# Query transposes for two heads at once and three moves of the order, in an encoder layer with attention and a state space

## The chip, the cores and the metric

The kernel runs on one core of one Trainium2 chip. The metric is the device time of one execution in microseconds (us), from several runs of the same program. Engines are named as in the profile: PE (TensorE; its weight loads stand apart as PEld), DVE (VectorE), ACT (ScalarE), POOL (GpSimd) and SP (SyncE, which here only issues transfers).

## The reference, cut to what matters

Two sequences of 512 tokens (1024 channels each, float32) go through one encoder layer: a projection, a windowed attention and a state-space branch side by side, a gated sum, and an MLP. The part that the change touches is the attention's queries:

```python
q = rms_norm(q.reshape(bsz, seq_len, N_HEADS, HEAD_DIM), q_gain)      # 16 heads of 64
k = rms_norm(k.reshape(bsz, seq_len, N_KV_HEADS, HEAD_DIM), k_gain)   # 4 key heads, 4 query heads each
s = jnp.einsum('nqkgd,njkd->nkgqj', qb, kw) * scale + bias            # a block of 128 queries, 3 blocks of keys
s = jnp.where(mask, s, NEG_INF)
p = softmax(concat([s, sink_col]))[..., :-1]
o = jnp.einsum('nkgqj,njkd->nqkgd', p, vw)
```

## The kernel before, in words

**Precision.** A float32 matmul is made of products of two rounded parts, high and low: each operand is split by ACT (a cast to the rounded type, the high part) and DVE (a subtraction, the low part).

**Stages around the change.** First the state-space scan, beside which PE computes gate columns. Then the *read-out* (lines 911 to 942): 32 iterations `q`, each with `turn_states` (copies on ACT and DVE), `read_out` (six matmuls of 128x128 on PE, lines 858 and 860), the load of tables for five iterations later (`tables_in`, on SP), pieces of other PE work (`work`: the last two gate columns in 12 pieces, then the key projection of 8 tiles in 16 pieces), and `gelu` (ACT, line 868), which frees the product's bank; there are two such banks. A table `casts` (line 906) says in which iterations a piece of the key weights (`w_k.piece`) or value weights (`w_v.piece`) is loaded (SP, line 717), cast (ACT, line 718) and subtracted (DVE, line 719). The pieces go through two raw buffers (`c_raw`). The first key product comes in iteration 14, by `until = (q + 1) * len(work) // NQ`, and with it the first two pieces are needed; pieces two and three are needed in iteration 15.

**Attention** (lines 953 to 1367). The loop runs over 8 steps (key head `j`, sequence `sq`); a step has four query blocks `qb` of 128 tokens. A `Unit` is one query block with its four heads: `scores` (two matmuls a head, of the queries against high and low keys), `largest` (DVE, line 1052: adds the bias and takes the row's maximum), `exp` (ACT, line 1058), then, one block later, `turn` (four transposes of p a key block, line 1064), `high` (ACT, line 1068), `low` (DVE, line 1073) and `value` (line 1080) for two or three key blocks, and `lower_part` and `add`. A block at the sequence's edge has two key blocks, others three; `n3` is their number for the block being finished, so it is 3 in the third and fourth blocks of a step (`qb` 2 and 3) and 2 in the first and second.

Beside a Unit the loop makes one `Tile` of the next step's queries: `project` (24 matmuls of 128x256 in parts of 8, 4, 2, 4, 4 and 2, line 724), `square` (ACT), `power` (DVE and POOL, lines 1005 to 1008), `norm`, `turn`, `high` and `low`, the last four one block later under the name `rows`. `norm` (DVE, line 1012) writes the normalized queries of four heads, and POOL (line 1013) copies them, so that each head stands twice, side by side. `turn` (line 1018) transposes each doubled head, 128x128, which puts a head's 64 channels twice under each other. `high` (ACT, line 1023) writes the scaled high part to both halves; `low` (DVE, line 1027) puts the low part over the lower half (partitions 64 to 127). One matmul then multiplies high and low queries with keys that stand twice as well. There are 32 tiles: three are finished before the loop (`entry`), the fourth in the first block of the first step, the others in the loop.

In a step's first block `key_copies` (POOL, line 972) and `key_turn` (lines 981 to 983) make the next step's keys ready, with PE, ACT and DVE in that order. In the second block `Divide` brings the row sums. In most steps a piece of the next query weights is loaded, cast and subtracted (lines 717 to 719) in two of the blocks; one step, in which all of them are in, has none.

**Order.** In read-out and attention the order on PE, ACT and DVE is that of the program text (`manual_schedule`), in attention POOL's too. An engine works in this order, and an instruction that waits holds all behind it. SP's order is not written out there: a planner issues a transfer where, by its own reckoning, the buffer is free.

Of the kernel before, what the change touches and what calls it, by code (L numbers as in the profile page):

```python
# [11 lines left out]
F32 = mybir.dt.float32  # L12
F32R = mybir.dt.float32r
I32 = mybir.dt.int32
AF = mybir.ActivationFunctionType
ALU = mybir.AluOpType
AX = mybir.AxisListType

P = 128
# [10 lines left out]
G = 4  # L30
HD = 64
# [32 lines left out]
def hybrid_layer(ctx, tc, x, xT, rel, onehot, early, w_qkv, w_ug, q_gain, k_gain, sink,  # L64
                 b_re, b_im, c_re, c_im, d_skip, w_glu, b_glu, w_out, ln2, w_up, w_down, out):
    nc = tc.nc
    V, S, PE, GP, SP = nc.vector, nc.scalar, nc.tensor, nc.gpsimd, nc.sync
# [12 lines left out]
    def acc():  # L80
        return ps_acc.tile([P, 512], F32, tag="acc", name="acc")
# [22 lines left out]
    ident = const.tile([P, P], F32, name="ident")  # L104
# [4 lines left out]
    gain_q = const.tile([P, 1], F32, name="gain_q")  # L109
# [161 lines left out]
    with tc.tile_pool(name="xin", bufs=2, reuse_waits="tile") as xin, tc.tile_pool(name="ssmc", bufs=1) as sc:  # L271
# [10 lines left out]
        rows, columns, first_w = {}, {}, []  # L282
# [191 lines left out]
        for n in (1, 2, 4):  # L474
            a, b = slice(1, n + 1), slice(n + 1, 2 * n + 1)
# [46 lines left out]
    if True:  # L522
        h = hp.tile([P, NCHUNK, 2, GROUPS, NSEQ], F32, name="h")
        GP.memset(h[:, 0], 0.0)

        with tc.tile_pool(name="ssmt", bufs=2) as sp:
# [64 lines left out]
            def turn(q, gp):  # L591
                bm = turned[gp] = sp.tile([P, 2, SH, P], F32, tag="bm", name="bm")
                ps = tps()
                for i in range(4):
                    PE.transpose(ps[:, i * P:(i + 1) * P],
                                 made[q][0][:, i // SH, gp * SH + i % SH].rearrange("p t c -> p (t c)"), ident)
                S.copy(bm.rearrange("p r g n -> p (r g n)"), ps)
# [56 lines left out]
            for q in range(NQ4):  # L654
                more = q + 1 < NQ4
                if q % 2 and more:
                    coefficients((q + 1) // 2)
                if q:
                    lags_out(q - 1)
                table_out(q)  # L660
                for gp in range(2):
                    turn(q, gp)
                if q % 2 == 0 and q:
                    lag_weights(q // 2)
                pay(act_owed)
                pay(cast_owed)
                if more:
                    tables(q + 1)
                run(3)
                pay(dve_owed)  # L670
                for gp in range(2):
                    states(q, gp)
                    if more:
                        inputs_in(q + 1, gp)
                lags(q)
                run(3)
                pay(act_owed)
                pay(dve_owed)
                if q % 2 and (q + 3) // 2 < KT:
                    bc_tiles[(q + 3) // 2] = b_and_c((q + 3) // 2)  # L680
# [88 lines left out]
    w_k = Block(w_qkv[K_BLK], [(knp, ("x_hi", "x_lo")), column])  # L769
    w_v = Block(w_qkv[V_BLK], [column, (evp, ("ev", "ev"))])  # L770

    with tc.tile_pool(name="ssmo", bufs=2, reuse_waits="tile") as sp:
# [129 lines left out]
        def last_cast():  # L902
            cast_owed.pop(0)()
            return dve_owed.pop()

        casts = {0: [last_cast], 1: [last_cast], 2: [lambda: w_k.piece(0)], 3: [lambda: w_k.piece(1)], 8: [lambda: w_k.piece(2)], 9: [lambda: w_k.piece(3)],
                 17: [lambda: w_v.piece(0)], 18: [lambda: w_v.piece(1)], 20: [lambda: w_v.piece(2)], 21: [lambda: w_v.piece(3)]}

        scan()
# [43 lines left out]
    with tc.tile_pool(name="att", bufs=2, reuse_waits="tile") as ap:  # L953
        steps = [(j, sq) for j in range(N_KV) for sq in range(NSEQ)]
        weights, keys, queries, biases = {0: w_q0}, {}, {}, {}
# [30 lines left out]
        class Tile:  # L986
# [6 lines left out]
            def project(self, n):  # L993
                (j, sq), col = self.key, self.t * P
                weights[j].multiply(self.ps, hT[sq], col, self.k, self.k + n)
                self.k += n
# [11 lines left out]
                GP.tensor_tensor(self.rq, ms, neg_half[:, 0:G], op=ALU.pow)  # L1008

            def norm(self):  # L1010
                self.qn = ap.tile([P, G, 2, HD], F32, tag="qn", name="qn")
                V.tensor_mul(self.qn[:, :, 0], self.psv, self.rq[:, :, None].to_broadcast([P, G, HD]))
                GP.tensor_copy(self.qn[:, :, 1], self.qn[:, :, 0])

            def turn(self):
                self.pt = acc()
                for h in range(G):
                    PE.transpose(self.pt[:, h * P:(h + 1) * P], self.qn[:, h].rearrange("p a d -> p (a d)"), ident)

            def high(self):  # L1020
                self.ptv = self.pt.rearrange("p (h t) -> p h t", h=G)
                self.dst = queries[self.key][:, :, self.t * P:(self.t + 1) * P]
                S.activation(self.dst, self.ptv, AF.Copy, scale=gain_q)

            def low(self):
                dst = self.dst[64:128]
                V.scalar_tensor_tensor(dst, self.ptv[64:128], gain_q[64:128], dst.bitcast(F32),
                                       op0=ALU.mult, op1=ALU.subtract)

        class Unit:  # L1030

# [98 lines left out]
        def entry():  # L1130
            load_biases(0)
            kd = key_copies(0, 0)
            for i in range(4):
                values(i)
                w_q0.piece(i)()
            old = None
            for t in range(4):
                new = Tile(0, 0, t)
                new.project(3 * KT)
                new.square()  # L1140
                if t == 0:
                    key_turn(0, 0, kd)
                if old:
                    old.turn()
                    old.high()
                    old.low()
                if t < 3:
                    new.power()
                values(4 + t)
                if t < 3:  # L1150
                    new.norm()
                    old = new
            return new
# [45 lines left out]
        if True:  # L1199
            rows = entry()  # L1200
            for i, (j, sq) in enumerate(steps):
# [8 lines left out]
                for qb in range(NB):  # L1210
                    if 1 <= i < 3:

                        t = (i - 1) * NB + qb
# [4 lines left out]
                    n3 = prev.nkb if prev else 0  # L1218
# [54 lines left out]
                    cur.largest(3)  # L1273
                    if n3 > 2:
                        prev.turn(2)
                        prev.high(2)
                    project(4)
                    if rows:
                        rows.turn()
                    if kd:  # L1280
                        key_turn(*nxt, kd)
# [35 lines left out]
                    owed, prev, rows = prev, cur, new  # L1317
# [173 lines left out]
    with tc.tile_pool(name="glu", bufs=2, reuse_waits="tile") as gpool:  # L1491
# [11 lines left out]
        def gate_in(m, low):  # L1503
            gs_, yr, ga, at = gated[m]
            S.activation(gs_, gs_, AF.Sigmoid)
            V.tensor_mul(at, at, ga)
            low()
            V.tensor_mul(gs_, gs_, yr)
# [27 lines left out]
        for m in range(1, KT):  # L1536
            col = ahead if m == 1 else Column(m)
            for s in range(NSEQ):
                col.multiply(max((s + 1) * 3 * KT - col.i, 0))
                subs = []  # L1540
                if s == 0:
                    if 3 <= m < KT - 1:
                        split_piece()
                    if 1 < m < KT - 1:
                        w_g[m + 1], subs = column_parts(m + 1)
                ending = m == KT - 1 and s
                if ending:
                    low = late()
                gl = bank_out(m, col.ps[s])
                if not ending:  # L1550
                    low = late()
                for sub in subs:
                    sub()
                gate = m if m < 3 and s == 0 else m + 1 if s and 2 <= m < KT - 1 else 0
                if gate:
                    gate_in(gate, low)
                else:
                    low()
                if s == 0 and m < KT - 1:
                    gated[m + 1] = loads(m + 1)  # L1560
                if s and 2 <= m < KT - 1:
                    load_piece(m - 2)
                    if m == KT - 2:
                        load_piece(m - 1)
                late = lambda m=m, s=s, gl=gl: mix(m, s, gl)
                if m == KT - 1:
                    load_piece(6 + s)
# [238 lines left out]
    with tc.tile_pool(name="up", bufs=2, reuse_waits="tile") as fp:  # L1806
# [29 lines left out]
        def entry_parts():  # L1836
            raw = slot_d.tile([P, 4, 2, HALF], F32, tag="act0", name="e_raw")
            part = slot_d.tile([P, 4, 2, HALF], F32R, tag="act1", name="e_part")
            SP.dma_start(raw[:, 0], a_scr[0, :, 0:2, :])
            SP.dma_start(raw[:, 1], w_down[0, 0, :, 0:2, :])  # L1840

            def high():
                for i in range(2):
                    S.copy(part[:, 2 * i], raw[:, i])

            def low():
                for i in range(2):
                    V.tensor_sub(part[:, 2 * i + 1], raw[:, i], part[:, 2 * i].bitcast(F32))

            return high, low, [[part[:, 0], part[:, 1]], [part[:, 2], part[:, 3]]]  # L1850

        for r in range(NPAIR):
# [12 lines left out]
            if last_r:  # L1865
                w2, w3, w1, w4_, w_a22 = [lambda p=w(): p for w in (w2, w3, w1, w4_, w_a22)]
                high, low, entry_hl = entry_parts()
                final = tc.manual_schedule(engines={mybir.EngineType.PE, mybir.EngineType.Activation, mybir.EngineType.DVE})
                final.__enter__()
# [3 lines left out]
            if last_r:  # L1873
                high()
# [185 lines left out]
```

## Time and profile before

| | us |
|---|---|
| median of 3 runs | 1469.36 |
| lowest, highest | 1468.56, 1470.11 |
| the profiled execution | 1469.22 |
| its span, first to last instruction | 1467.4 |
| PE busy in the span | 1446.3 |
| DVE busy | 1094.6 |
| ACT busy | 764.2 |
| POOL busy | 168.9 |

Some 1.8 us of the execution lie outside the span. The granted TensorE clock was 0.999 of full speed over the span. A row of the profile names engine, line, operation and tiles (written <- read), the shape, a count, busy time and the mean of one in ns, and the engine's idle time before it with what ended it. A timeline row starts with start and length in us from the span's start. PE's matmuls are pipelined and their ends are modelled, so their cost is read from start to start.

### The profile page before, as it was taken

What the parts mean: (1) busy time and instruction counts of PE and PEld (TensorE: products, weight loads), DVE (VectorE), ACT (ScalarE), POOL (GpSimd) and SP (SyncE); (2) the same over time, 40 slices, a digit from 0 to 9 for tenths busy, and PEclk for the clock granted to TensorE, in tenths of its full rate; (3) what the DMA queues carried; (4) which work ended last, traced back from release to release, by engine and by line L of the source; (5) the groups of instructions that cost most, each with busy time, mean ns of one, the idle gap of its engine ahead of it and who ended that gap; (6) DMA issues with size and microseconds to landing.
All of it is one profiled execution on the core that took longest, in us unless ns stands there. A gap on an engine that the chain in (4) does not pass through costs nothing.

```text
span 1467.4 us, 21580 instructions
## 1 busy us (share of the span) xinstructions
PE 1446.3 (99%) x7782; PEld 1234.1 (84%) x7782; DVE 1094.6 (75%) x1836; ACT 764.2 (52%) x1366; POOL 168.9 (12%) x270
## 2 busy tenths in 40 slices
PE   6999999999999999999999999999999999999998
PEld 5888888888999899987888888888888888888887
DVE  7799979975636889888974689877776588575653
ACT  5489862233426778787532355554554444333332
POOL 4111120000223333343101000000000000000000
PEclk9999999999999999999999999999999999999999
DMA  8355567259941413236964134544443894454441
GB/s 300 112 171 174 161 206 268 101 178 290 307 131 35 121 46 89 95 130 217 303 212 144 72 115 165 174 149 147 155 158 123 302 346 147 158 177 153 129 129 58
DMA packets 129239, 243.86 MB, mean 166 GB/s; under 512 B 16060, under 2 KB 59324, under 8 KB 129133
## 3 DMA queue, kind: packets, MB, share of 16 engines
q1 hardware_dynamic: 104684, 186.87, 40.4%
q10 hardware_dynamic: 21888, 46.15, 8.3%
q0 software_dynamic: 2560, 9.48, 2.0%
q8 instruction: 61, 1.00, 0.3%
q14 instruction: 46, 0.37, 0.1%
HBM read 173.20 MB, written 81.82 MB: 174 GB/s over the span
## 4 chain that ended last, share of the span: by engine, by line
PE 91%; DVE 3%; ACT 2%; DMA 1%; issue 1%; POOL 1%; SPq 0%; DVEq 0%; ACTq 0%; POOLq 0%
PE bank L115 14%; PE bank L116 14%; PE bank L117 14%; PE acc L141 11%; PE acc L724 8%; PE acc L753 5%; PE acc L115 3%; PE acc L117 3%; PE acc L116 3%; PE po L1080 2%; PE sps L604 2%; PE sps L1048 2%; PE sps L860 2%; PE tps L1064 2%; PE lag L619 1%
## 5 line engine op out<-in xcount | busy, mean ns | idle before, releaser
L116 PE MATMUL bank<-b_lo,a_hi 128*128 128x512 f32 x440 | 171.2, 389 | 0.0
L117 PE MATMUL bank<-b_hi,a_lo 128*128 128x512 f32 x440 | 171.2, 389 | 0.0
L115 PE MATMUL bank<-b_hi,a_hi 128*128 128x512 f32 x440 | 171.2, 389 | 0.0
L724 PE MATMUL acc<-w_hi,hT 128*128 128x256 f32 x768 | 165.0, 291 | 0.0
L141 PE MATMUL acc<-hT,c_hi 128*128 128x512 f32 x512 | 161.1, 394 | 0.0
L1933 ACT CAST a_hi<-d_a 128x1024 fp32r<-128x1024 f32 x55 | 58.0, 1054 | 178.1 <-PE bank L116 175.2
L1934 DVE TENSOR_TENSOR a_lo<-d_a,a_hi 128x1024 fp32r<-128x1024 f32 x55 | 67.3, 1223 | 99.4 <-ACT a_hi L1933 97.3
L724 PEld LDWEIGHTS acc<-w_hi,hT 128*128 128x128 f32 x768 | 126.7, 190 | 1.7
L141 PEld LDWEIGHTS acc<-hT,c_hi 128*128 128x128 f32 x512 | 94.6, 188 | 21.0 <-issue 2.5
L724 PE MATMUL acc<-w_lo,hT 128*128 128x256 f32 x384 | 108.2, 282 | 0.0
L141 PE MATMUL acc<-hT,c_lo 128*128 128x512 f32 x256 | 100.3, 392 | 0.0
L115 PE MATMUL bank<-act,u_hi 128*128 128x512 f32 x256 | 99.6, 389 | 0.0
L116 PE MATMUL bank<-act,u_hi 128*128 128x512 f32 x256 | 99.6, 389 | 0.0
L117 PE MATMUL bank<-act,u_lo 128*128 128x512 f32 x256 | 99.6, 389 | 0.0
L117 PEld LDWEIGHTS bank<-b_hi,a_lo 128*128 128x128 f32 x440 | 82.6, 188 | 17.3
L115 PEld LDWEIGHTS bank<-b_hi,a_hi 128*128 128x128 f32 x440 | 82.6, 188 | 17.1
L116 PEld LDWEIGHTS bank<-b_lo,a_hi 128*128 128x128 f32 x440 | 82.6, 188 | 17.1
L1058 ACT ACTIVATE p<-p,nmx 128x257 f32<-128x257 f32 (+1 forms) x128 | 72.1, 564 | 27.0 <-DVE nmx L1052 24.3
L724 PEld LDWEIGHTS acc<-w_lo,hT 128*128 128x128 f32 x384 | 73.0, 190 | 2.5
L1052 DVE CUSTOM_DVE_ANT_0 p<-sps,bias,nsink 128x256 f32<-128x256 f32 (+1 forms) x128 | 69.2, 541 | 2.9 <-PE sps L1048 0.4
L1717 ACT CAST u_hi<-s 128x512 fp32r<-128x512 f32 x64 | 39.3, 621 | 59.8 <-PE bank L116 43.1
L1934 DVE TENSOR_TENSOR b_lo<-k,b_hi 128x1024 fp32r<-128x1024 f32 x55 | 66.9, 1217 | 0.0
(387 smaller groups left out, 3622.9 us busy)
## 6 DMA issues: line engine op xcount, KB each, us to landing
d_a<-a_scr SPq DMA_DIRECT2D x55, 512.0 KB, 3.6
u_raw<-in_w_up_dram SPq DMA_DIRECT2D x32, 512.0 KB, 5.7
a_scr<-t ACTq DMA_DIRECT2D x64, 256.0 KB, 2.1
k<-in_w_down_dram SPq DMA_DIRECT2D x32, 512.0 KB, 5.7
a_scr<-a ACTq DMA_DIRECT2D x48, 256.0 KB, 3.3
c_raw<-in_w_ug_dram SPq DMA_DIRECT2D x44, 256.0 KB, 3.6
ct_scr<-ctab SPq DMA_DIRECT2D x16, 576.0 KB, 3.3
ctab_in<-ct_scr SPq DMA_DIRECT2D x32, 288.0 KB, 4.7
```

The source lines that it names most:

```text
L115: PE.matmul(ps, a[0], b[0], start=first, stop=False)
L116: PE.matmul(ps, a[0], b[1], start=False, stop=False)
L117: PE.matmul(ps, a[1], b[0], start=False, stop=last)
L141: PE.matmul(self.ps[s], self.w[p == 2][:, k, :], hT[s][p == 1][:, k, :], start=i % (3 * KT) == 0, stop=i % (3 * KT) == 3 * KT - 1)
L604: PE.matmul(ps[:, i * P:(i + 1) * P], bm[:, ri, g, :], u_sb[:, g, :], start=True, stop=True)
L724: PE.matmul(ps, act[p == 2][:, k, col:col + P], self.w[k // 4][p == 1][:, k % 4, :], start=i == 0, stop=i == 3 * KT - 1)
L753: PE.matmul(self.ps[s], w_g[self.m][p == 2][:, k, :], y_part(s, int(p == 1), k), start=k + p == 0, stop=k == KT - 1 and p == 2)
L1052: V.tensor_tensor_reduce(self.p[:, h, 1:1 + self.nk], self.s[h][:, 0:self.nk], biases[self.j][h][:, b0:b0 + self.nk], -1.0, nsink[:, hh:hh ...
L1058: S.activation(p, p, AF.Exp, bias=self.nmx[:, h:h + 1], scale=-1.0, accum_out=self.sums[:, h, self.qb:self.qb + 1])
L1717: S.copy(hi, src)
L1933: S.copy(hi, src)
L1934: V.tensor_sub(lo, src, hi.bitcast(F32))
```

## The change

1. `norm` writes four heads once, without the copy on POOL. `turn` transposes two neighbouring heads in one 128x128 block, so two transposes make a tile and the even head lies in partitions 0 to 63, the odd one in 64 to 127. `high` and `low` become two instructions each, one for even and one for odd heads, of 64 partitions and 256 elements: the high part stays in its half, the low part is written to the other half. For even heads the queries' layout is as before, for odd heads high and low have changed places; the keys stand twice, so the product is the same.
2. The four key pieces of the read-out are cast in iterations 4, 6, 9 and 11 instead of 2, 3, 8 and 9.
3. Where `n3` is 3, `rows.turn()` comes right behind `prev.turn(2)`, ahead of four projection matmuls; elsewhere its place is the old one.

```diff
-        casts = {0: [last_cast], 1: [last_cast], 2: [lambda: w_k.piece(0)], 3: [lambda: w_k.piece(1)], 8: [lambda: w_k.piece(2)], 9: [lambda: w_k.piece(3)],
+        casts = {0: [last_cast], 1: [last_cast], 4: [lambda: w_k.piece(0)], 6: [lambda: w_k.piece(1)], 9: [lambda: w_k.piece(2)], 11: [lambda: w_k.piece(3)],
...
             def norm(self):
-                self.qn = ap.tile([P, G, 2, HD], F32, tag="qn", name="qn")
-                V.tensor_mul(self.qn[:, :, 0], self.psv, self.rq[:, :, None].to_broadcast([P, G, HD]))
-                GP.tensor_copy(self.qn[:, :, 1], self.qn[:, :, 0])
+                self.qn = ap.tile([P, G, HD], F32, tag="qn", name="qn")
+                V.tensor_mul(self.qn, self.psv, self.rq[:, :, None].to_broadcast([P, G, HD]))
 
             def turn(self):
                 self.pt = acc()
-                for h in range(G):
-                    PE.transpose(self.pt[:, h * P:(h + 1) * P], self.qn[:, h].rearrange("p a d -> p (a d)"), ident)
+                for m in range(G // 2):
+                    PE.transpose(self.pt[:, m * P:(m + 1) * P], self.qn[:, 2 * m:2 * m + 2].rearrange("p a d -> p (a d)"), ident)
 
             def high(self):
-                self.ptv = self.pt.rearrange("p (h t) -> p h t", h=G)
-                self.dst = queries[self.key][:, :, self.t * P:(self.t + 1) * P]
-                S.activation(self.dst, self.ptv, AF.Copy, scale=gain_q)
+
+                q = queries[self.key][:, :, self.t * P:(self.t + 1) * P].rearrange("p (m e) t -> p m e t", e=2)
+                pt = self.pt[:, 0:G // 2 * P].rearrange("p (m t) -> p m t", m=G // 2)
+                self.halves = []
+                for e, (own, other) in enumerate(((slice(0, 64), slice(64, P)), (slice(64, P), slice(0, 64)))):
+                    hi, lo, src = q[own, :, e], q[other, :, e], pt[own]
+                    S.activation(hi, src, AF.Copy, scale=gain_q[own])
+                    self.halves.append((hi, lo, src, gain_q[own]))
 
             def low(self):
-                dst = self.dst[64:128]
-                V.scalar_tensor_tensor(dst, self.ptv[64:128], gain_q[64:128], dst.bitcast(F32),
-                                       op0=ALU.mult, op1=ALU.subtract)
+                for hi, lo, src, gain in self.halves:
+                    V.scalar_tensor_tensor(lo, src, gain, hi.bitcast(F32), op0=ALU.mult, op1=ALU.subtract)
...
                     if n3 > 2:
                         prev.turn(2)
+                        if rows:
+                            rows.turn()
                         prev.high(2)
                     project(4)
-                    if rows:
+                    if rows and n3 < 3:
                         rows.turn()
```

## The prediction

> **What bounds the kernel now.** I read the page's busy shares first, then the stretches of the two stages that the edits touch, then the groups of instructions there, the waits, and last the timeline around each moved instruction. The page:
>
> ```profile
> span 1467.4 us, 21580 instructions
> PE 1446.3 (99%) x7782; PEld 1234.1 (84%) x7782; DVE 1094.6 (75%) x1836; ACT 764.2 (52%) x1366; POOL 168.9 (12%) x270
> ```
>
> PE is busy for 99% of the span, so a matmul taken away is worth its time unless another engine is late just there. Where that is so, the average hides. The stretches (width, then busy us and count of PE, PEld, DVE, ACT, POOL): ten us of the read-out; one step of the attention loop (545.5 to 574.1); of that step the part from the second query block to the end of the third; a step without weight casts.
>
> ```profile
> 335.00:345.00 10.00, 8.62 (x52) 7.20 (x51) 6.47 (x9) 5.02 (x9) 0.00 (x0) 1.00 0.83 267
> 545.50:574.10 28.60, 28.56 (x213) 26.71 (x212) 25.28 (x67) 23.13 (x59) 10.15 (x18) 1.00 0.29 85
> 546.30:559.00 12.70, 12.66 (x92) 11.51 (x90) 12.49 (x33) 10.65 (x28) 3.46 (x7) 1.00 0.25 73
> 602.20:630.50 28.30, 28.26 (x213) 26.52 (x211) 24.07 (x65) 22.22 (x58) 10.15 (x18) 1.00 0.20 60
> ```
>
> In the loop PE looks full and DVE is at 25.28 of 28.60 us; but from 546.3 to 559.0 DVE is busy 12.49 of 12.70 us (98%). There two engines bound the time together, and relieving PE alone gains little. In the other half of a step DVE has room. In the read-out PE stands still for 10.00 - 8.62 = 1.4 us.
>
> **Paired transposes, on PE.** The groups that the edit changes or resembles:
>
> ```profile
> L1018 PE MATMUL acc<-ident,qn 128*128 128x128 f32 x128 | 19.7, 277 | 1.2 <-POOL qn L1013 1.2
> L1013 POOL COPY qn<-qn 128x256 f32<-128x256 f32 x32 | 12.7, 398 | 29.7 <-DVE qn L1012 25.5 <-PE sps L1048 3.6 <-PE tps L1064 0.6
> L1023 ACT ACTIVATE qa<-acc,gain_q 128x512 fp32r<-128x512 f32 x32 | 21.6, 675 | 0.1
> L1027 DVE SCALAR_TENSOR_TENSOR qa<-acc,gain_q,qa 64x512 fp32r<-64x512 f32 x32 | 24.2, 757 | 20.2 <-ACT qa L1023 20.0
> L149 ACT ACTIVATE sg<-acc 128x512 f32<-128x512 f32 x16 | 9.6, 599 | 36.0 <-PE acc L141 35.9
> L868 ACT ACTIVATE ysb<-sps 128x256 f32<-128x256 f32 x32 | 12.2, 381 | 11.2 <-PE sps L860 9.5 <-ACT ysb L868 0.9 <-DMA u_sb<-u_scr 0.4
> L1052 DVE CUSTOM_DVE_ANT_0 p<-sps,bias,nsink 128x384 f32<-128x384 f32 x64 | 38.6, 603 | 1.0
> L1052 DVE CUSTOM_DVE_ANT_0 p<-sps,bias,nsink 128x256 f32<-128x256 f32 x64 | 30.6, 479 | 1.9 <-PE sps L1048 0.4 <-PE acc L1018 0.4
> L1090 DVE TENSOR_TENSOR ya<-po,ol 64x256 f32<-64x256 f32 x64 | 26.4, 412 | 0.4
> ```
>
> There are 128 query transposes, four for each of 32 tiles; two of each four go. What one costs is its pitch, not its 277 ns. This is the end of the third query block (start, length, engine, line):
>
> ```profile
> 557.37 0.60 PE L1018 MATMUL acc<-ident,qn 128*128 128x128 f32 x4
> ...
> 558.16 0.28 PE L724 MATMUL acc<-w_lo,hT 128*128 128x256 f32 x1
> ...
> 558.27 0.68 DVE L1073 TENSOR_TENSOR pl<-tps,ph 128x512 fp32r<-128x512 f32 x1
> 558.28 0.40 PE L724 MATMUL acc<-w_hi,hT 128*128 128x256 f32 x2
> 558.39 0.62 ACT L1058 ACTIVATE p<-p,nmx 128x385 f32<-128x385 f32 x1 [0.56 <-DVE nmx L1052]
> ...
> 559.00 0.67 ACT L1023 ACTIVATE qa<-acc,gain_q 128x512 fp32r<-128x512 f32 x1
> ...
> 559.22 0.39 PE L1080 MATMUL po<-pl,va 128*128 128x512 f32 x1
> ...
> 559.71 0.76 DVE L1027 SCALAR_TENSOR_TENSOR qa<-acc,gain_q,qa 64x512 fp32r<-64x512 f32 x1 [0.75 <-ACT qa L1023]
> ```
>
> Four take 0.60 us, so the pitch is (0.60 - 0.277) / 3 = 0.108 us. A tile saves 0.216 us of PE, 32 tiles 6.9 us. That is the ceiling of this edit on PE.
>
> **Paired transposes, on ACT and DVE.** The one scaled copy of 128x512 becomes two of 64x256, the one subtraction of 64x512 two of 64x256. No row shows these forms. For ACT, 512 against 256 elements is 599 against 381 ns, 0.85 ns an element, so a half costs 675 - 218 = 457 ns (bounds: 338, half of the row, and 675), two 914, 0.24 us more a tile. For DVE, 384 against 256 is 603 against 479 ns, 0.97 ns an element, so a half costs 757 - 248 = 509 ns. The nearest row by shape is the 64x256 sum at 412 ns. Extra DVE a tile, called x from here: 0.07 by that row, 0.26 by the slope, and between 0 (half price) and 0.76 (full price) at the extremes. I take x = 0.26, since the subtraction with a factor is costlier at 512 (757 ns) than the plain subtraction beside it (0.68 us, above). ACT has room for its 0.24 (23.13 of 28.60 us). The chain from copy to subtraction hardly grows, as the first subtraction can run beside the second copy: 0.457 + 2 x 0.509 = 1.48 against 0.675 + 0.757 = 1.43, +0.05. If ACT's cover failed, that chain would cost 0.24 instead.
>
> **Where PE's saving stays.** A step has four tiles, one for each query block. The end of the second block:
>
> ```profile
> 551.99 0.76 DVE L1027 SCALAR_TENSOR_TENSOR qa<-acc,gain_q,qa 64x512 fp32r<-64x512 f32 x1
> 552.78 0.62 DVE L1052 CUSTOM_DVE_ANT_0 p<-sps,bias,nsink 128x384 f32<-128x384 f32 x1
> ...
> 551.99 0.62 ACT L1058 ACTIVATE p<-p,nmx 128x385 f32<-128x385 f32 x1 [0.15 <-DVE nmx L1052]
> 552.52 0.19 ACT L1058 ACTIVATION_READ_ACCUMULATOR p<-p,nmx 128x1 f32 x1
> ...
> 552.75 0.60 PE L1064 MATMUL tps<-ident,p 128*128 128x128 f32 x4
> ```
>
> The last exponential, itself waiting for DVE, ends at 552.52 + 0.19 = 552.71, and PE transposes its result at 552.75, with 0.04 to spare. PE that comes 0.216 earlier just waits: the second block's saving is lost. One subtraction of queries lies inside the DVE run (551.99), so the run ends x later: the last low part of p ends at 558.95 + 0.26 = 559.21 where PE needs it at 559.22. The slack of 0.27 is used up, and the third block's saving is lost too, with about 0.1 on top for the +0.05 and a semaphore. The fourth and first blocks keep theirs: DVE idles there (0.75 in the row at 559.71), and the chain over the next keys starts from PE itself. So:
> - three tiles before the loop, with nothing beside them: 3 x 0.216 = 0.65
> - first blocks, 8 x 0.216 = 1.73; fourth blocks, 7 x 0.216 = 1.51
> - second and third blocks: kept only in the step without weight casts: 2 x 0.216 = 0.43; lost in six steps, with 6 x 0.1 = -0.6. The casts' DVE work in an ordinary step and in that one (1.37 us against none, of 24.07 in 28.30 busy):
>
> ```profile
> 545.00:574.00 29.00, 1.37 (x2) 1.00 0.29 83
> 603.00:632.00 29.00, 0.00 (x0) 1.00 0.20 58
> ```
>
> Against this edit speaks the Trainium skill, page "VectorE: DVE Perf Modes", section "Two Vector instructions with no wait between them": an instruction whose source or target starts in another 32-partition quarter than the last one's starts only when that has ended, and both halves now cross over. The trace agrees: behind the subtraction (end 551.99 + 0.76 = 552.75), which writes to another quarter than its successor, that one starts at 552.78 and not before the end. My x lays the halves end to end, so by the rule the sum stands; if the second half could start 0.1 early, x would be 0.16 and six third blocks would lose 0.1 less, 1462.5.
>
> **The copy on POOL** (398 ns) goes, and with it a link ahead of each transpose. PE waited for it, and for the key copy queued behind it on POOL:
>
> ```profile
> 455.60 0.66 PE L1018 MATMUL acc<-ident,qn 128*128 128x128 f32 x4 [0.82 <-POOL qn L1013]
> 484.89 0.66 PE L981 MATMUL tps<-ident,kd 128*128 128x128 f32 x4 [0.37 <-POOL kd L972]
> 655.54 0.66 PE L1018 MATMUL acc<-ident,qn 128*128 128x128 f32 x4 [0.36 <-POOL qn L1013]
> ```
>
> 0.40 of the first, 0.37 and 0.36 can go: 1.13, called 1.1. Next late behind the first is DVE's scaling of the queries.
>
> **Transposes moved ahead of four matmuls** in the third and fourth blocks: the same work, 0. They need the scaled queries about 0.48 us sooner (four 256-wide matmuls at the 0.12 between 558.16 and 558.28), which the missing copy returns nearly whole (0.40). Queued behind a late one would be the four projections and the products with the values; the price then is under 0.1 a tile.
>
> **Later key casts.** The read-out now (the load's issue, the cast behind it, the Gelu behind that, PE):
>
> ```profile
> 330.14 0.41 SPq L717 DMA_DIRECT2D w_raw<-in_w_qkv_dram  x1
> ...
> 336.10 0.62 ACT L718 CAST w_hi<-w_raw 128x512 fp32r<-128x512 f32 x1 [5.70 <-DMA w_raw<-in_w_qkv_dram]
> 336.63 0.38 ACT L868 ACTIVATE ysb<-sps 128x256 f32<-128x256 f32 x1
> ...
> 337.06 0.49 PE L858 MATMUL sps<-u_sb,toep 128*128 128x128 f32 x2 [0.61 <-ACT ysb L868]
> ...
> 338.31 0.68 PE L860 MATMUL sps<-st,ctab_in 128*128 128x128 f32 x4 [0.77 <-ACT st L845]
> ```
>
> ```profile
> L868 ACT ACTIVATE ysb<-sps x32: 375/382/389, 328.2 to 415.6; 128x256 f32<-128x256 f32 x32
> ```
>
> ACT stands 5.70 us at the first cast for its load, the Gelu behind it comes late, and PE waits 0.61 + 0.77 = 1.4 us. The Gelus' first and last start give an iteration (415.6 - 328.2) / 31 = 2.8 us. Two iterations later the load has landed (336.0 against some 336.1 - 5.7 + 5.6 = 336.0), if it is issued where it is now: SP's order isn't written by hand, and the buffer is free as early as before. Each moved piece carries a load on SP, a cast (0.62 us, covered by ACT's 5.02 of 10.00) and a subtraction (DVE 6.47 of 10.00); the first use of the weights is in iteration 14, the last cast now in 11. Gain 1.4; bounds: a loss of 4 x 1.4 - 1.4 = 4.2 if each of the four waits so, and a gain of 1.4.
>
> Sum: 0.65 + 1.73 + 1.51 + 0.43 - 0.6 + 1.1 + 1.4 = 6.2 us. The profiled execution took 1469.22 us; the median of 1469.36 is 0.14 above it. Forecast: 1463.1.
>
> **Rivals.**
> - *All is kept* (x near 0, the run's ends move with PE): 6.9 + 1.1 + 1.4 = 9.4, giving 1459.9. For it: the 412 ns row. Against: 12.49 of 12.70.
> - *The load moves with the cast.* SP issues it later, and ACT waits again. One such wait: 1463.1 + 1.4 = 1464.5; at all four casts 1463.1 + 4 x 1.4 = 1468.7. For it: 5.70 us to land at a DMA share of 0.83. Against: the load was issued at 330.14, well ahead of its cast, so it follows its buffer.
> - *The change does not relieve the loop*: DVE holds all blocks, only the tiles before the loop, POOL and read-out count: 0.65 + 1.1 + 1.4 - 0.6 = 2.5, giving 1466.9.
> - *Slower: DVE becomes the loop's bound.* If a half subtraction costs as much as a whole, x = 0.76: a step has 25.28 + 4 x 0.76 = 28.3 us of DVE work and two waits of 0.75 for ACT that nothing fills, 29.8 against 28.6. Seven steps lose 8.5, the rest gains 3.3 (0.65 + 1.1 + 1.4, and 0.2 behind the last step's first block): 1474.6. It decides from x = (28.60 - 25.28 - 1.5) / 4 + 3.3 / 28 = 0.57, a half at 0.66 us. Against: both pairs of rows show time falling with elements.
>
> **How the numbers follow.** Chances: forecast 0.52, all kept 0.18, load moved 0.12, loop not relieved 0.11, slower 0.07. A measurement of this kernel tells 0.2%, 2.9 us, from no change, so faster means under 1466.4. The forecast, all kept, most of load moved and a little of the fourth case give 0.80; same 0.13; slower 0.07. The range leaves out the slower case, the tail of the moved load and the edge of all kept: 1459.0 to 1467.2.
>
> **What would show it.** 64 query transposes, none on POOL behind L1012; halves near 457 and 509 ns; no wait of ACT over 1 us at the key casts and PE full from 335 to 345; in a step with weight casts a saving of some 0.3 us, in the one without 0.8; new PE waits for the last exponential and low part of p in the second and third blocks. Halves over 0.66 us, or ACT waits at iterations 4 to 11, would prove the sum wrong.

## The result, and the profile after

The changed kernel takes 1475.05 us (median of 5 runs, 1474.51 to 1476.42), against 1469.36 before: a ratio of 1.0041, interval 1.0027 to 1.0055. It is slower by 5.7 us; the forecast was 1463.1. The profiled execution has a span of 1473.3 us, 5.9 more than before, at a granted clock of 1.0.

The page after, its span, its busy shares and its chain of work by engine:

```profile
span 1473.3 us, 21484 instructions
PE 1444.3 (98%) x7718; PEld 1226.7 (83%) x7718; DVE 1100.5 (75%) x1868; ACT 775.6 (53%) x1398; POOL 153.8 (10%) x238
PE 82%; DVE 7%; issue 3%; ACT 3%; DMA 3%; POOL 1%; SPq 0%; DVEq 0%; POOLq 0%; ACTq 0%
```

PE has 64 matmuls fewer and yet the span is longer: PE now waits. In the chain the share of PE is 82%, where before it was this:

```profile
PE 91%; DVE 3%; ACT 2%; DMA 1%; issue 1%; POOL 1%; SPq 0%; DVEq 0%; ACTq 0%; POOLq 0%
```

The stretches that were shown of before (width, then busy us and count of PE, PEld, DVE, ACT, POOL): the read-out; from the second query block to the end of the third; one step, and for that step the one of before between the same two events (from the third head's score matmul in a step's second block to the same one a step later).

```profile
335.00:345.00 10.00, 10.00 (x64) 8.95 (x63) 5.67 (x8) 3.79 (x7) 0.00 (x0) 1.00 0.99 306
546.50:559.40 12.90, 12.20 (x84) 10.68 (x82) 12.70 (x34) 10.98 (x28) 2.73 (x6) 1.00 0.27 70
547.19:576.56 29.37, 28.41 (x202) 25.70 (x202) 25.83 (x71) 24.42 (x63) 8.58 (x14) 1.00 0.29 82
```

```profile
546.99:575.37 28.38, 28.34 (x209) 26.49 (x210) 25.08 (x67) 22.91 (x59) 10.15 (x18) 1.00 0.29 85
```

In the read-out PE is full, as forecast. A step takes 29.37 us instead of 28.38, though PE has no more to do in it (202 matmuls for 209) and DVE only 0.75 us more: DVE, busy 25.83 of 29.37, has 3.5 us free, and PE is idle for 1.0. Neither engine is full, so waits between them must close the step; the experiments below test which.

The changed groups, after (busy us in all, mean ns of one, idle time before it):

```profile
L1017 PE MATMUL acc<-ident,qn 128*128 128x128 f32 x64 | 12.3, 273 | 0.4 <-DVE qn L1012 0.4
L1026 ACT ACTIVATE qa<-acc,gain_q 64x256 fp32r<-64x256 f32 x64 | 29.6, 463 | 0.5
L1031 DVE SCALAR_TENSOR_TENSOR qa<-acc,gain_q,qa 64x256 fp32r<-64x256 f32 x64 | 30.9, 483 | 26.7 <-ACT qa L1026 25.2 <-PE sps L1051 0.8
```

The halves cost 463 and 483 ns, near the 457 and 509 forecast. But DVE stands 25.2 us ahead of the subtractions for ACT's copies, against 20.0 before. The end of the first query block, after (start, length, engine, line):

```profile
572.81 0.69 ACT L982 ACTIVATE kh<-tps,gain_k 128x512 fp32r<-128x512 f32 x1 [0.36 <-PE tps L981]
573.40 0.50 ACT L1061 ACTIVATE p<-p,nmx 128x257 f32<-128x257 f32 x1
573.89 0.94 ACT L1026 ACTIVATE qa<-acc,gain_q 64x256 fp32r<-64x256 f32 x2
574.86 0.98 DVE L1031 SCALAR_TENSOR_TENSOR qa<-acc,gain_q,qa 64x256 fp32r<-64x256 f32 x2 [0.58 <-ACT qa L1026]
575.88 0.62 DVE L1055 CUSTOM_DVE_ANT_0 p<-sps,bias,nsink 128x384 f32<-128x384 f32 x1
576.56 0.44 PE L1051 MATMUL sps<-kh,qa 128*128 128x384 f32 x1 [0.52 <-DVE nmx L1055]
```

The same place before:

```profile
572.11 0.69 ACT L982 ACTIVATE kh<-tps,gain_k 128x512 fp32r<-128x512 f32 x1 [0.88 <-PE tps L981]
573.19 0.68 ACT L1023 ACTIVATE qa<-acc,gain_q 128x512 fp32r<-128x512 f32 x1
573.90 0.76 DVE L1027 SCALAR_TENSOR_TENSOR qa<-acc,gain_q,qa 64x512 fp32r<-64x512 f32 x1 [0.32 <-ACT qa L1023]
574.69 0.62 DVE L1052 CUSTOM_DVE_ANT_0 p<-sps,bias,nsink 128x384 f32<-128x384 f32 x1
575.37 0.45 PE L1048 MATMUL sps<-kh,qa 128*128 128x384 f32 x1
```

This is where half of a step's loss arises. The row at 573.89 is *both* copies, 0.94 us; the subtractions begin at 574.86, when both are done, and take 0.98. From the copy's start to the end of the subtraction it was 1.47 us (573.19 to 574.66) and is 1.95 (573.89 to 575.84). Behind the subtraction, in DVE's written order, stands the next block's first maximum, and PE's third scores in that block wait for it. PE waited for nothing there; now it waits 0.52 us. From the key copy to those scores it was 3.26 us (572.11 to 575.37) and is 3.75.

The waits of the loop (444 to 690 us), first after, then before (engine, line, waited for: us in all, times, longest):

```profile
PEld po L1083 <- DVE pl L1076: 11.8, 38, 0.5
PEld sps L1051 <- DVE nmx L1055: 9.8, 17, 1.4
PE sps L1051 <- DVE nmx L1055: 6.3, 14, 1.2
```

```profile
PEld po L1080 <- DVE pl L1073: 3.9, 12, 0.5
PEld sps L1048 <- DVE nmx L1052: 2.1, 7, 0.7
PE sps L1048 <- DVE nmx L1052: 0.5, 1, 0.5
```

The matmuls' own waits for a maximum, 0.5 us in all before, are 6.3; their weight loads' waits for p's low part have tripled.

Where the 5.9 us of the two profiled spans lie, by the start of each block's first score matmul: the loop begins 2.98 us earlier (451.36 to 448.38); its first seven steps are 6.3 longer together, some 1.2 of it in two blocks that also wait for a load (they come up at twice_pe); the last step 0.9; 1.3 come where PE waits behind the loop, and 0.4 later. The wait behind the loop is taken up at the end. In a steady step the four blocks, from first scores to first scores, have these lengths, here with those of the experiments:

| us | first | second | third | fourth | step |
|---|---|---|---|---|---|
| before | 6.48 | 7.36 | 7.41 | 7.14 | 28.4 |
| after | 6.50 | 7.84 | 7.52 | 7.50 | 29.4 |
| halves_only | 6.53 | 7.63 | 7.46 | 7.52 | 29.1 |
| twice_pe | 6.51 | 7.84 | 7.55 | 7.73 | 29.6 |
| defer_low | 6.97 | 8.11 | 8.54 | 7.91 | 31.5 |
| after_sooner | 6.27 | 7.84 | 7.52 | 6.73 | 28.4 |
| after_sooner_kd | 6.27 | 6.98 | 7.53 | 6.74 | 27.5 |
| twice_sooner_kd | 6.47 | 7.00 | 7.56 | 6.95 | 28.0 |
| before_sooner | 6.47 | 7.36 | 7.41 | 6.94 | 28.2 |
| before_sooner_kd | 6.48 | 6.61 | 7.40 | 6.96 | 27.4 |

The second block is longer by 0.48, just what the chain at the first block's end grew by.

### The profile page after: what moved, and what is told of

It is laid out like the page before. It is cut to its first block, busy times and chain, and to the rows that moved or that the text cites. A ratio compares the mean times of both kernels' runs of the same rounds, so it can differ in the third digit from the quotient of the medians.

```text
span 1473.3 us, 21484 instructions
## 1 busy us (share of the span) xinstructions
PE 1444.3 (98%) x7718; PEld 1226.7 (83%) x7718; DVE 1100.5 (75%) x1868; ACT 775.6 (53%) x1398; POOL 153.8 (10%) x238
## 4 chain that ended last, share of the span: by engine, by line
PE 82%; DVE 7%; issue 3%; ACT 3%; DMA 3%; POOL 1%; SPq 0%; DVEq 0%; POOLq 0%; ACTq 0%
PE bank L116 14%; PE bank L115 13%; PE bank L117 13%; PE acc L141 12%; PE acc L724 5%; PE acc L115 3%; PE acc L117 3%; PE acc L116 3%; PE acc L753 3%; PE sps L604 2%; PE sps L860 2%; DVE p L1055 1%; DVE qa L1031 1%; PE lag L619 1%; ACT qa L1026 1%
## 5 line engine op out<-in xcount | busy, mean ns | idle before, releaser
L1061 ACT ACTIVATE p<-p,nmx 128x257 f32<-128x257 f32 (+1 forms) x128 | 72.2, 565 | 29.4 <-DVE nmx L1055 27.9
```

Source lines behind the costliest of these rows:

```text
L1061: S.activation(p, p, AF.Exp, bias=self.nmx[:, h:h + 1], scale=-1.0, accum_out=self.sums[:, h, self.qb:self.qb + 1])
```

## The experiments

Theory A: the chain of both copies, both subtractions and the next block's first maximum closes the second and fourth blocks, and its growth is the loss. Rival C: the transposes moved ahead of four matmuls cost it. Rival D: it is DVE's added work, wherever it stands. Other rivals are named where they come up. Ratios are to the kernel before on the same chip; nomove, twice_sooner_kd and before_sooner_kd ran on another chip than the rest, where the kernel before takes 1468.89 us and not 1469.39 to 1469.64, so their ratios are what to compare.

**The casts alone (casts_only)**: before, with the new line of `casts` and nothing else.

> The kernel before with the later key casts alone. Theory A (the later casts are a gain, and what made the change slower lies in the attention loop): the 1.4 us for which PE stood still at iterations 3 and 4 of the read-out go, nothing else moves, 1469.4 - 1.4 = 1468.0 or a little less. Rival B (the later casts move transfers on SP and cost later, for instance the 1.5 us wait near 720 us of the changed kernel): the read-out gains 1.4 and the column stage loses 1.5, no change, 1469.4.

1467.2 us, ratio 0.9985 (0.9977 to 0.9994): 2.2 us faster. This edit does what was forecast of it (1.4 lies in the interval of 0.9 to 3.4), and B falls.

**The paired transposes alone (pair_only)**: the edits of `norm`, `turn`, `high` and `low`, with the old casts and the transposes in their old place.

> The kernel before with the paired transposes alone (old casts, old place of the transposes). Theory A (the halves lengthen the chain exponential, copy, subtraction, maximum by 0.48 us, and the loop waits for it): as slow as the changed kernel and 1.4 more for the read-out's wait, 1476.5. Rival C (the moved transposes are what costs): 1463 to 1466.

1475.75 us, ratio 1.0041 (1.0028 to 1.0053). The whole loss is in this edit, and C falls: nothing was moved here. (That this kernel lacks the gain of the later casts and still has the ratio of the changed kernel lies within the intervals.)

**The third edit undone (nomove)**: after, with `rows.turn()` at its old place in every block.

```diff
                         prev.turn(2)
-                        if rows:
-                            rows.turn()
                         prev.high(2)
                     project(4)
-                    if rows and n3 < 3:
+                    if rows:
                         rows.turn()
```

> The changed kernel with the query transposes at their old place in all blocks (the third edit undone). Theory A (the copies wait for the fourth exponential anyway, so it doesn't matter when PE has turned the queries): the loop's steps stay at 29.4, 1475.0 within 1. Rival C (the moved transposes hold PE up): 1472 or less.

1474.24 us, ratio 1.0037 (1.0023 to 1.0051), the loop's steady steps as after (29.36). The move costs and gains nothing that shows, as forecast.

**Halves without pairs (halves_only)**: before, with copy and subtraction each cut in two, four transposes and the doubled queries kept. The high copies are 128x256, the subtractions 64x256.

```diff
-                S.activation(self.dst, self.ptv, AF.Copy, scale=gain_q)
+                for m in range(2):
+                    S.activation(self.dst[:, 2 * m:2 * m + 2], self.ptv[:, 2 * m:2 * m + 2], AF.Copy, scale=gain_q)
```

`low` has the same loop over its one subtraction. The rival here: cutting in two costs little, and it is the crossing of high and low parts to other partitions that costs.

> The kernel before with its copy and its subtraction of the queries each cut into two halves (heads 0 and 1, heads 2 and 3) and nothing else: 128 transposes, the copy on POOL, old casts. Theory A (the two halves, run one after the other as copy, copy, subtraction, subtraction, cost 0.48 us between the last exponential and the next block's first maximum): the loop's blocks lengthen as in the changed kernel, 0.48 + 0.11 + 0.36 a step, 7 steps, 1469.4 + 6.7 = 1476. Rival G (the pairing itself costs: the writes across partitions, or the earlier transposes): 1469.4 to 1471.

1474.51 us, ratio 1.0035 (1.0023 to 1.0048): nearly all of the loss, without any crossing, if 1.5 us less than A gave. The place, in this kernel:

```profile
574.33 0.83 ACT L1024 ACTIVATE qa<-acc,gain_q 128x256 fp32r<-128x256 f32 x2
575.19 0.89 DVE L1030 SCALAR_TENSOR_TENSOR qa<-acc,gain_q,qa 64x256 fp32r<-64x256 f32 x2 [0.47 <-ACT qa L1024]
```

Two copies in 0.83 and then two subtractions in 0.89: a chain of 1.75 us, 0.28 longer than before, and the second block is 0.27 longer. The crossing adds the rest: 0.94 and 0.98 in the changed kernel, 0.20 more, and a second block 0.21 longer. (In the fourth block, 7.52 here and 7.50 in the changed kernel, the crossing's 0.20 and PE's saving of 0.216 cancel by this count.)

**The subtraction put later (defer_low)**: after, with `rows.low()` behind the next block's second maximum.

```diff
-                        rows.low()
+                        late_rows = rows
...
                     cur.largest(1)
+                    if late_rows:
+                        late_rows.low()
+                        late_rows = None
```

> The changed kernel with the two subtractions of the queries put behind the second maximum of the next query block on DVE: the same work, off the chain that ends in the next block's first maximum. Theory A (chain): a step of the loop falls from 29.4 to about 28.1 us or less, 7 steps, 1475.1 - 9 = 1466. Rival D (DVE simply has 0.21 us more work a tile and is full): the work stays, so no change, 1475.

1488.32 us, ratio 1.0126 (1.0111 to 1.0141). Both expectations missed. The waits of PE for a maximum are gone from the loop, as A has it, but these stand in their place:

```profile
PEld po L1083 <- DVE pl L1076: 33.8, 43, 1.4
PE po L1083 <- DVE pl L1076: 21.6, 34, 1.1
DVE p L1055 <- PE sps L1051: 18.6, 24, 1.1
```

At its new place the pair of subtractions (0.98 us) stands ahead of p's low part, which PE needs at once; and at its old place DVE now stands idle, 18.6 us in all for PE's scores. In the third block, where next to nothing of the pair was on the path (7.41 before, 7.52 after), it costs its whole length (7.52 to 8.54); in the others 0.27 to 0.47 is left of it. The old place was a gap: only what stuck out of it was on the path. So this run does not decide between A and D.

**PE's saving given back (twice_pe)**: after, with each query transpose done twice, so that PE has as much work as before.

```diff
                 for m in range(G // 2):
-                    PE.transpose(self.pt[:, m * P:(m + 1) * P], ...
+                    for _ in range(2):
+                        PE.transpose(self.pt[:, m * P:(m + 1) * P], ...
```

The rival: PE still sets the time in the loop, and the saving is in the 1475.

> The changed kernel with each of the two transposes of a tile done twice (PE has its old 128 back, the result is the same). Theory A (in the loop PE waits for the chain, its saving is lost): most of it is hidden in PE's waits, 0.65 us before the loop and 1 to 2 in the loop, 1476 to 1477.5. Rival E (PE is the bound all along, something else cost 12 us): the whole 64 x 0.108 = 6.9 us come back, 1482.

1474.71 us, ratio 1.0033 (1.002 to 1.0045): no slower than after, and less than either expectation. The second and third blocks don't feel it (0.03 at most); the fourth takes 0.23 more, the first up to 0.27 in some steps, so that most steps are 0.2 to 0.5 longer, of the 0.86 given back. In the two profiled executions this doesn't show in the span, since two blocks of the kernel after wait for loads and those of this one don't. The third block of the second step takes 9.00 us there instead of 7.52, behind this wait of ACT for weights:

```profile
494.86 0.62 ACT L718 CAST w_hi<-w_raw 128x512 fp32r<-128x512 f32 x1 [1.79 <-DMA w_raw<-in_w_qkv_dram]
```

The second block of the third step takes 8.48 instead of 7.84, behind a wait of DVE of 1.08 us for a bias. Eleven of the 13 traces have a wait for weights of 0.9 to 2.2 us in that third block of the second step. Whether it spared the executions of this kernel that weren't profiled is not shown; what PE's saving is worth is better read from the blocks.

**The copies sooner, third and fourth blocks (after_sooner)**: in the second block the copy of the queries stands ahead of the last exponential already (`sooner`); here in the third and fourth too.

```diff
-                    sooner = rows and n3 == 2 and not kd
+                    sooner = rows and not kd
```

> The changed kernel with the two copies of the queries ahead of the fourth exponential in the third and fourth blocks too, as they already are in the second. Theory A (it is the wait of the subtractions for the copies behind the exponential): the subtractions start right behind the last low part of p, the wait for the maximum in the fourth block (0.31 us with what follows it) goes, block 3 falls from 7.50 to 7.14 or less, 7 steps: 1475.0 - 3 = 1472. Rival D (DVE's 0.21 us more a tile cost wherever they stand): 1475.

1466.99 us, ratio 0.9983 (0.9974 to 0.9992): 8 us faster than after by one line, more than A expected. The work on every engine is that of the changed kernel, so rival D falls. The fourth block goes from 7.50 to 6.73 and the first, behind it, from 6.50 to 6.27; the second, whose chain is untouched, stays at 7.84.

**And in the first block (after_sooner_kd)**: there, where the keys are turned too (`kd`), copies and subtractions stand ahead of the key turn.

```diff
                     if rows and n3 < 3:
                         rows.turn()
+                        if kd:
+                            rows.high()
+                            rows.low()
                     if kd:
                         key_turn(*nxt, kd)
...
-                    if rows:
-                        if not sooner:
-                            rows.high()
+                    if rows and not kd:
                         rows.low()
```

The rival: the keys come later, and that costs as much.

> As the kernel with the copies ahead of the fourth exponential, and in a step's first block copies and subtractions ahead of the key turn as well. Theory A: also the 0.67 us wait in the second block shrinks, block 1 falls from 7.84 to 7.4, 7 x 0.44 = 3 more: 1469. Rival H (the key turn's copy and subtraction, now late, take the place of the wait): 1472, as without it.

1461.99 us, ratio 0.9948 (0.9935 to 0.9961). The second block falls from 7.84 to 6.98, by 0.86 where 0.44 was expected. What the order does is seen at the end of the third block, where the copies now come ahead of the exponential:

```profile
552.23 0.95 ACT L1026 ACTIVATE qa<-acc,gain_q 64x256 fp32r<-64x256 f32 x2
553.21 0.62 ACT L1061 ACTIVATE p<-p,nmx 128x385 f32<-128x385 f32 x1
553.49 0.98 DVE L1031 SCALAR_TENSOR_TENSOR qa<-acc,gain_q,qa 64x256 fp32r<-64x256 f32 x2
```

The same place in the kernel after, where the exponential is first, and PE's third scores behind it:

```profile
558.82 0.62 ACT L1061 ACTIVATE p<-p,nmx 128x385 f32<-128x385 f32 x1 [0.56 <-DVE nmx L1055]
559.43 0.94 ACT L1026 ACTIVATE qa<-acc,gain_q 64x256 fp32r<-64x256 f32 x2
560.40 0.98 DVE L1031 SCALAR_TENSOR_TENSOR qa<-acc,gain_q,qa 64x256 fp32r<-64x256 f32 x2 [1.02 <-ACT qa L1026]
561.96 0.39 PE L1051 MATMUL sps<-kh,qa 128*128 128x256 f32 x1 [0.15 <-DVE nmx L1055]
```

The halves are as long as they were; DVE no longer waits for them (1.02 us after), and PE no longer waits for the maximum behind them.

**That order in the kernel before (before_sooner)**: single copies and four transposes, with the later casts, the moved transposes and the line of after_sooner.

> The kernel before with the later casts, the transposes right behind p's third block, and the copy of the queries ahead of the fourth exponential in the third and fourth blocks: four transposes, one copy, one subtraction. Theory A with PE as the bound of these blocks in the old layout: no more than the casts give, 1467.2. If the old layout too waits for the subtraction there: 1465.

1467.2 us, ratio 0.9984 (0.9975 to 0.9993), as expected, and no faster than casts_only. In the blocks only the fourth gains, 0.15 to 0.22 in three of the seven steps: with the shorter chain less stuck out of the gap. This fits what after_sooner gained beyond its expectation: for the fourth block, 6.94 here less PE's 0.216 is 6.72, and 6.73 was measured; for the first, 6.47 less 0.216 is 6.25, and 6.27 was measured. So with the chain out of the way PE's saving shows in both.

**The transposes twice, in the new order (twice_sooner_kd)**: after_sooner_kd with the loop of twice_pe. If PE sets a block's time there, the block takes 0.216 us more.

> The kernel with copies ahead of the exponential and of the key turn (1462.0), with each transpose of the queries done twice: PE has its 128 back. Theory A (with the chain out of the way PE binds the first and fourth blocks, DVE's unbroken run the second and third): blocks 0 and 3 lengthen by 0.22 each, 7 x 0.43 + 0.65 before the loop, 1465.7. If PE bound all four blocks: 1462 + 6.9 = 1468.9. If DVE bound all four: 1462.7.

1464.1 us, ratio 0.9966 (0.9954 to 0.9979). First and fourth blocks 0.20 and 0.21 longer, second and third 0.02 and 0.03, as A has it. With the chain out of the way PE's saving is kept in two blocks of four.

**The whole new order in the kernel before (before_sooner_kd)**: as before_sooner, with the copy and the subtraction of the first block ahead of the key turn as well. The rival here: the order is all there is to gain, and pairs add nothing.

> The kernel before (four transposes, one copy, one subtraction, the copy on POOL) with the later casts and the same new order: transposes behind p's third block, copy and subtraction ahead of the exponential and of the key turn. Theory A: PE binds it, about as the kernel with doubled transposes but with 0.21 us less DVE a tile, 1465 to 1466; so the pairing is worth 3 to 4 us once the order fits. Rival: the order is all there is to gain, 1462.

1461.13 us, ratio 0.995 (0.9937 to 0.9962). A's expectation fell and the rival held: without pairs the kernel is as fast as with them (ratio 0.9948). The pairs save 0.21 and 0.22 us in the first and fourth blocks, and lose 0.37 and 0.13 in the second and third, the two that PE's transposes don't set. That the added time of the halves is what lengthens those two was not tested apart. This and after_sooner_kd are faster than both kernels.

## Why the prediction was wrong

**The step that failed** is the sentence "The chain from copy to subtraction hardly grows, as the first subtraction can run beside the second copy: 0.457 + 2 x 0.509 = 1.48 against 0.675 + 0.757 = 1.43, +0.05." The first subtraction doesn't run beside the second copy. In all 32 tiles of the changed kernel it starts 0.032 us or more behind the *second* copy's end, and never sooner than 0.51 behind the first's; in halves_only too the least distance from the second is 0.032. In 30 of the 32 tiles only the second copy signals in the trace. The chain grew by 0.48, ten times the term. Both copies and both subtractions touch the same tiles, of which one is a bank that both engines read; which of them makes the program wait for both copies was not tried and stays open.

**The cover.** The prediction gave a price for the failure of ACT's cover, 0.24, and put it nowhere in the sum. It also took DVE's idle 0.75 us ahead of the subtraction for room. It is the opposite: DVE waits there for a chain that goes on behind it, over the next block's first maximum to PE's scores. Time added to that chain is added to the block, however idle DVE is before it.

**Where PE's saving stays.** "The fourth and first blocks keep theirs" failed with it: 1.73 + 1.51 were counted there, and the fourth block lost 0.36 instead, the first 0.02. In the fourth PE's 0.216 does count (given back in twice_pe, it costs 0.23), but the chain took more than it gave. The second block was to lose its saving and little more, and lost 0.48; the third was to lose 0.1 and lost 0.11. That these two keep nothing of PE's saving was right, but the sum let them keep 0.43 in the step without weight casts, and there they lost 0.15 and 0.11; that step is 0.63 longer (28.13 to 28.76). Neither of the signs that were to prove the sum wrong, halves over 0.66 us and waits of ACT at the key casts, appeared: the sum failed at a wait that it had not looked for.

**What was right.** The ceiling: 0.216 a tile, which twice_sooner_kd measures again as 0.20 and 0.21 where PE sets the time. The halves, 463 and 483 ns for 457 and 509. The later casts, 2.2 us for 1.4: the first load is issued at 329.68, no later than before, its cast waits for no load, and PE's stall is gone. The last row, of the Gelus, gives the read-out's length, 327.8 to 413.2, against 328.2 to 415.6:

```profile
329.68 0.41 SPq L717 DMA_DIRECT2D w_raw<-in_w_qkv_dram  x1
337.35 0.62 ACT L718 CAST w_hi<-w_raw 128x512 fp32r<-128x512 f32 x1 [0.42 <-ACT ysb L868]
341.41 0.62 ACT L718 CAST w_hi<-w_raw 128x512 fp32r<-128x512 f32 x1 [0.45 <-ACT ysb L868]
L868 ACT ACTIVATE ysb<-sps x32: 372/380/390, 327.8 to 413.2; 128x256 f32<-128x256 f32 x32
```

The moved transposes, nothing. What lies ahead of the loop was to give 0.65 + 1.4 = 2.05 us and gave 2.98, and the traces divide it. The read-out, from its first Gelu to its last, takes 87.35 us before and 85.44 after, 1.9 less; it is 85.4 in all ten kernels with the later casts, and 86.7 to 87.4 in the three without. From the last Gelu to the loop's first scores it is 35.79 before and 35.14 after: the 0.65 of the three tiles, just as forecast, and 35.79 again in twice_pe. The other 0.43 lie ahead of the read-out, which no edit touches, and where halves_only is 0.94 sooner than before.

The missing copy on POOL was to give 1.1 in three blocks of the loop. PE's wait of 0.82 us at the first of them is now one of 0.4 for the scaling of the queries, as written, and that block (the loop's first) falls from 6.02 to 5.20, to 5.42 in twice_pe. The second step's first block falls from 7.36 to 6.94, but the last step's, the third of the three, grows from 6.58 to 6.74.

**The rule of the Trainium skill** that the prediction set against the pairs (page "VectorE: DVE Perf Modes", section "Two Vector instructions with no wait between them") agrees with the runs and has a price here: two subtractions with sources and targets that start in one quarter take 0.89 us together (halves_only), two that cross take 0.98, end to end as the sum had laid them. The 0.1 that the prediction gave for a second half that starts early was right (0.09), but it is the smaller part of what was missed.

**The slower rival** gave 1474.6, near the time that came, but by another mechanism: it needed halves of 0.66 us or more, and they take 0.483.

**Not foreseen and not explained**: 1.3 us of the loss lie behind the loop, where the chain of waits after runs through a transfer of the last row factors:

```profile
700.72 9.71 DMA fac<-rs_scr
710.65 2.83 POOL ya L1122
713.76 4.43 DMA mix_scr<-ya
718.32 0.69 DVE w L1398
720.71 0.70 DVE c_lo L737
721.45 2.57 PE acc L753 x10
```

Here PE stands idle for 1.15 us, waiting for DVE, and before it didn't. The wait differs from kernel to kernel (defer_low 1.19, pair_only 0.95, nomove 0.66, casts_only 0.46, twice_pe 0.45, before_sooner_kd 0.41, after_sooner_kd 0.09, the others none), without following any one edit. Why the transfer takes 9.7 us was not tried.

## What to carry to other kernels

An engine's idle time ahead of an instruction is room only if nothing that sets the time hangs behind that instruction; where it is the last link of a chain to the busiest engine, follow the chain from its first link and add all that the change puts into it. When one instruction becomes two on each of two engines, do the sum with all of the first engine's ahead of all of the second's, unless a trace shows the overlap. And ask whether the order can take such a chain out of the way before taking work off the busiest engine: here one line that moves a copy was worth 8 us, and with the whole new order 64 transposes less were worth nothing (ratios 0.9948 with the pairs and 0.995 without).

## What the runs showed of the hardware

A PE that is busy for 99% of its span (1442.8 of 1460.6 us in twice_sooner_kd) set the time in two blocks of four: 0.216 us of transposes added to each block lengthened the first and fourth by 0.20 and 0.21, the second and third by 0.02 and 0.03. And a subtraction pair of 0.98 us, moved out of a gap into DVE's unbroken run, made the kernel 13.3 us slower (1488.32 against 1475.05), though the work is the same: half of the 27.4 us that 28 pairs take.
